# Attention output from float32r products with both parts of the values as 128 weight columns

## The chip, the cores and the metric

The kernel runs on one core of a Trainium2 chip. The metric is the device time of one execution in microseconds. Before the change it was 3017.5 us, the median of three runs (3017.45 to 3017.97). The engines are TensorE (PE; its weight loads are listed apart as PEld), VectorE (DVE), ScalarE (ACT), GpSimd (POOL) and SyncE (SP, which issues the DMAs).

## The reference

The program is a mixing block with a gated delta rule (block 1) and, behind it, a two-layer block (block 2) for 512 tokens of width 1024. Each layer of block 2 is a feed-forward part, a mixer, a second feed-forward part and a gated embedding. The change lies in the mixer's attention, eight heads of width 64:

```python
def forgetting_attention(q, k, v, f_logit):
    b, s, h, dh = q.shape
    scale = 1.0 / float(np.sqrt(dh))
    c = jnp.cumsum(jax.nn.log_sigmoid(f_logit.astype(jnp.float32)), axis=1)
    ...
    for blk in range(s // Q_BLOCK):
        qs, qe = blk * Q_BLOCK, (blk + 1) * Q_BLOCK
        sc = jnp.einsum('bhqd,bhkd->bhqk', qh[:, :, qs:qe], kh[:, :, :qe]).astype(jnp.float32) * scale
        sc = sc + (c[:, :, qs:qe, None] - c[:, :, None, :qe])
        causal = jnp.arange(qs, qe)[:, None] >= jnp.arange(qe)[None, :]
        sc = jnp.where(causal[None, None], sc, -jnp.inf)
        pr = jax.nn.softmax(sc, axis=-1).astype(vh.dtype)
        outs.append(jnp.einsum('bhqk,bhkd->bhqd', pr, vh[:, :, :qe]))
```

Everything is float32. The query block is 128 tokens, so four blocks see 128, 256, 384 and 512 keys. The change concerns the last line, probabilities times values.

## The kernel before

Weight products are made from two-part operands: a float32 matrix is split into hi, its value rounded to float32r, and lo, the rest in float32r, and three float32r matmuls add hi·hi, hi·lo and lo·hi (`mm3`, lines 153 to 158). Weights stream from HBM in the order of their use; ScalarE casts four tiles to `whi` (line 108) and VectorE subtracts to get `wlo` (line 109). A matmul of 512 moving columns into one PSUM bank is the usual piece.

In the mixer the tokens' values are computed first, token-major, in four PSUM banks `v` (lines 499 to 506); ScalarE copies each bank to SBUF in float32 with a scale per token (`vt`, line 509). Then come the forget gates (line 512, their product is `pj`), the first pair's queries and keys, and then `heads` for the four pairs of heads. For a pair it makes, for each of the four query blocks, the scores of both heads `sc` (lines 451, 453, the mask 457), the row maxima (VectorE, line 459), the exponentials (ScalarE, line 461), the reciprocal and the scaling of the probabilities `pe` (VectorE, lines 462, 466). Then, for each of four key blocks, it transposes the probabilities on TensorE into a PSUM bank `pt` (line 476), copies that to SBUF on VectorE (line 480), and multiplies values by them (`o`, line 484). These last products are in plain float32: 64 columns of values are the weights, the transposed probabilities of 512, 384, 256 or 128 queries move, and the two heads write the lower and the upper 64 partitions of one bank. At the end ScalarE and VectorE split the output into `oh` and `ol` (lines 168, 169).

Between these steps stand fillers. `fill(n)` advances the projection of the next pair's queries and keys (`qk_steps`; the last pair has the first of the later gates) by n steps of three weight products, and `taps(n)` gives VectorE n multiply-adds of the depthwise convolution (`cy`, line 418), which nobody needs before the attention is over. The finished order on each engine is settled when the program is built: a scheduler goes through the instructions by their place in the code and by when their operands and buffers are expected to be ready. Each engine then works through its own list in order. PSUM is divided into four banks for accumulators (`acc`: v, pj) and four for the rest (`aux`: sc, pt, and o before the change).

After the four pairs come sixteen gates and the output projections; the attention's output is needed after the first four gates.

Of the kernel before, what the change touches and what calls it, by code (L numbers as in the profile page):

```python
# [7 lines left out]
F32 = mybir.dt.float32  # L8
F32R = mybir.dt.float32r
AF = mybir.ActivationFunctionType  # L10
ALU = mybir.AluOpType
# [12 lines left out]
ENG2 = dict(pe="v", dup="a", pt="vv")  # L24
# [58 lines left out]
class Stream:  # L83
    """Weight tiles in the order of their use: loads of GRP tiles, split in units of UNIT tiles."""
# [40 lines left out]
    def group(self, dst):  # L125
        """the next GRP tiles as they are"""
        assert self.i % GRP == 0
        self.nc.sync.dma_start(dst, self.dram[self.i // GRP])
        self.i += GRP
# [31 lines left out]
def split_scaled(nc, hi, lo, src, scale):  # L161
    """hi + lo == src * scale (scale: a value per partition)."""
    nc.scalar.activation(hi, src, AF.Copy, scale=scale)
    nc.vector.scalar_tensor_tensor(lo, src, scale, hi.bitcast(F32), op0=ALU.mult, op1=ALU.subtract)
# [12 lines left out]
def block2(tc, kk, W, h, xp, x0, sq0, p_t, par, out_t):  # L177
    """h: 8 tiles [128, 512] (features on partitions), short of the factor 1 / rms of the block before.
    x0: the first operand, split. sq0: the sums of squares for that factor and for the first norm."""
    nc = tc.nc  # L180
    with ExitStack() as ctx:
# [23 lines left out]
        # second operands of the scores, double buffered, for the two heads of a pair:  # L205
        # upper q and ones; lower k and both parts of the decay sums
# [9 lines left out]
        # mt[q, k] = NEG where k > q  # L216
# [60 lines left out]
        def token_sums(sq):  # L277
            """means of squares with a token per partition, [128, chunk]"""
# [14 lines left out]
        def spread(r):  # L293
            """from a token per partition to tokens along the free axis of every partition"""
# [6 lines left out]
        def first_norm():  # L301
            """1 / rms of the block before times the first norm's factor; and the former for h"""
# [57 lines left out]
        def mixer(l, after):  # L360
# [8 lines left out]
            def qk_steps(hp, qk1):  # L369
                """for either head: (upper | lower) q and (upper | upper) k"""  # L370
# [56 lines left out]
            def taps(n):  # L427
                """the next n of the products that are possible by now"""
# [7 lines left out]
            def heads(hp, qk1, filler):  # L436
                """heads 2 hp and 2 hp + 1, each in its half of the partitions"""
# [31 lines left out]
                po_ = paux("o")  # L469
                for kb in range(4):  # L470
                    n = S - kb * P
                    pts = []
                    for i in range(2):
# [4 lines left out]
                        t = mtile(8 + kb % 2 * 4 + 2 * i, "pt", F32)[:, :n]  # L478
                        copy = nc.scalar.copy if ENG2["pt"][i] == "a" else nc.vector.tensor_copy
                        copy(t, ps[:, :n])  # L480
                        pts.append(t)
                    fill(FILL[4 + kb])
                    for i, r in enumerate(rr):
                        nc.tensor.matmul(po_[r, kb * P:], lhsT=vt[kb][:, hp * P + 64 * i:hp * P + 64 * i + 64], rhs=pts[i],  # L484
                                         start=kb == 0, stop=kb == 3)
                split(nc, oh[hp], ol[hp], po_)
# [4 lines left out]
            # token sums of squares per partition, for the token-major values  # L491
# [6 lines left out]
            # v, token-major  # L498
# [8 lines left out]
            vt = [mtile(t, f"vt{t}", F32) for t in range(4)]  # L507
            for t in range(4):
                nc.scalar.activation(vt[t], vps[t], AF.Copy, scale=Rt[:, 2 * t:2 * t + 1])
            taps(TAPSV)  # L510
            # forget gates: rows 0..7 and again 64..71
# [9 lines left out]
            # -log_sigmoid = ln(1 + exp(-|z|)) - min(z, 0)  # L521
# [35 lines left out]
            # the merge: gates run ahead of the two parts  # L557
# [96 lines left out]
def blocks(v, n):  # L654
    """[..., n * 128] -> [128, ... * n]"""
# [43 lines left out]
# (shift, scale) blocks that are computed together  # L699
# [98 lines left out]
def block1(tc, kk, W, h, xp, hp, xt, ctxt, par1, po, rcnt, prep2):  # L798
    """Fills h (8 tiles [128, 512]) with the block's output before its final norm is applied, times the
    final gain; prep2(m) is called for each one. Returns the sums of squares for both norms."""  # L800
    nc = tc.nc
    with ExitStack() as ctx:
# [36 lines left out]
        # ---- constants  # L839
# [6 lines left out]
        for d in range(2):  # L846
            t = tmp("tri", (P, P))
            # d = 0: 1 where row <= col; d = 1: 1 where row >= col
# [7 lines left out]
        for b in (16, 32, 64):  # L856
            # -1 on the two off-diagonal blocks of every pair of b x b blocks
# [13 lines left out]
        # row selector: column r picks rows r and 64 + r  # L871
# [17 lines left out]
        # ---- modulation vectors, [128, block, (x, ctx)]  # L889
        # (x, ctx) of every input tile, the last ones filled up to a column tile  # L890
# [4 lines left out]
        # sums over the four column tiles, whose first two rows count  # L895
# [7 lines left out]
        def modulation(bs, tiled, tiles):  # L903
            """four blocks; tiled: with the inputs spread over four column tiles"""
# [19 lines left out]
        # ---- load x, ctx; sums of squares; scale by the reciprocal rms  # L924
# [21 lines left out]
        def newton(r, v, s):  # L946
            """r = 1 / sqrt(v) to float32's accuracy from an estimate r; s: scratch"""
# [80 lines left out]
        # ---- gates: per token on partitions, [128, chunk, 2 directions x 8 heads]  # L1028
# [50 lines left out]
        # ---- per head  # L1079
        # tokens with two columns of zeros around each sequence: ctx from 2 on, x from 260 on  # L1080
# [8 lines left out]
        def conv5(px, pc, blk, dst):  # L1089
            """centred convolution over tokens, then silu; dst: [128, NT + 2] (a gap after ctx) or [128, NX],  # L1090
            None: left in the input's place"""
# [25 lines left out]
        def k_in(hd):  # L1117
# [25 lines left out]
            # gamma and its product with the decay to the chunk's end, [128, chunk, direction]  # L1143
# [19 lines left out]
        def q_in(st):  # L1163
# [10 lines left out]
            # 128 eps (|q|^2 + eps)  # L1174
# [402 lines left out]
```

## Time and profile before

| | before |
|---|---|
| median of the runs | 3017.5 us |
| span of the profiled execution | 3016.3 us |
| TensorE busy | 2970.0 us (98%) |
| VectorE busy | 1916.6 us (64%) |
| ScalarE busy | 1302.3 us (43%) |
| o (L484), chain that ended last | 1% of the span |

The median of the runs is 1.2 us above the profiled span. The busy time of an engine is the sum of the stretches in which it executes; the chain that ended last follows the work back from the last instruction, and shows which engine was waited for. A layer's attention is about 3% of the span, so its own windows say more than the shares of the whole. Time between two starts on an engine is its price when it works without a gap; the time shown for one instruction is longer, since the next begins before it has drained.

### The profile page before, as it was taken

The numbers are of one execution on the slowest core, as the hardware profiler recorded it, in microseconds if no ns is written. First come the engines' busy times: TensorE is split into PE (matmuls) and PEld (weight loads), VectorE is DVE, ScalarE is ACT, GpSimd is POOL, SyncE is SP. The second block draws the span as 40 slices with busy tenths as digits, with TensorE's granted clock in tenths as the row PEclk, the third lists the DMA queues.
The fourth block names the chain that finished last, engine by engine and source line by source line (L and its number), as shares of the span: only waits on it lengthen the run. The fifth ranks groups of instructions, "written<-read, shape, count | busy, mean of one in ns | idle before, by whom it ended". The sixth has DMA issues, their size and how long they took to land.

```text
span 3016.3 us, 37957 instructions
## 1 busy us (share of the span) xinstructions
PE 2970.0 (98%) x13980; PEld 2395.5 (79%) x13980; DVE 1916.6 (64%) x3778; ACT 1302.3 (43%) x2395; POOL 48.4 (2%) x105
## 2 busy tenths in 40 slices
PE   7999999999999999999999999999999999999998
PEld 4888887777888887688888878888887688888886
DVE  5788888777534469886543447434469886543446
ACT  5667666435323335544332335323335544432333
POOL 1000000000000000000000000000000000000000
PEclk9999999999999999999999999999999999999999
DMA  5211113232232232133333333323222123233322
GB/s 199 66 46 45 52 51 110 91 91 89 93 98 97 92 98 78 50 92 97 94 95 98 98 98 93 96 91 98 91 93 89 50 85 98 93 96 98 98 91 84
DMA packets 112971, 268.77 MB, mean 89 GB/s; under 512 B 43537, under 2 KB 47121, under 8 KB 112785
## 3 DMA queue, kind: packets, MB, share of 16 engines
q1 hardware_dynamic: 111760, 266.28, 28.3%
q8 instruction: 110, 1.80, 0.2%
q14 instruction: 77, 0.62, 0.1%
q0 software_dynamic: 1024, 0.07, 0.0%
HBM read 262.17 MB, written 4.06 MB: 88 GB/s over the span
## 4 chain that ended last, share of the span: by engine, by line
PE 95%; DVE 2%; ACT 2%; issue 1%; DMA 0%; DVEq 0%; SPq 0%; ACTq 0%
PE pj L158 17%; PE pj L157 17%; PE pj L156 17%; PE fo L158 5%; PE fo L157 5%; PE fo L156 5%; PE px L156 3%; PE px L157 3%; PE px L158 3%; PE o L484 1%; PE wo L157 1%; PE wo L158 1%; PE mP L1266 1%; PE mX L1261 1%; PE wo L156 1%; PE chn L1313 1%
## 5 line engine op out<-in xcount | busy, mean ns | idle before, releaser
L108 ACT CAST whi<-wraw 128x512 fp32r<-128x512 f32 x914 | 566.6, 620 | 1191.9 <-PE pj L157 712.2
L109 DVE TENSOR_TENSOR wlo<-wraw,whi 128x512 fp32r<-128x512 f32 x914 | 627.1, 687 | 465.9 <-ACT whi L108 441.8
L157 PE MATMUL pj<-xl,whi 128*128 128x512 f32 x1712 | 673.0, 393 | 0.0
L156 PE MATMUL pj<-xh,whi 128*128 128x512 f32 x1712 | 670.7, 392 | 0.9 <-DVE h L1502 0.9
L158 PE MATMUL pj<-xh,wlo 128*128 128x512 f32 x1712 | 670.0, 391 | 0.0
L158 PEld LDWEIGHTS pj<-xh,wlo 128*128 128x128 f32 x1712 | 322.1, 188 | 68.1 <-issue 2.3
L157 PEld LDWEIGHTS pj<-xl,whi 128*128 128x128 f32 x1712 | 322.2, 188 | 67.9 <-issue 2.7
L156 PEld LDWEIGHTS pj<-xh,whi 128*128 128x128 f32 x1712 | 322.4, 188 | 66.8 <-ACT whi L108 1.3
L158 PE MATMUL fo<-gh,wlo 128*128 128x512 f32 x704 | 279.1, 396 | 0.0
L157 PE MATMUL fo<-gl,whi 128*128 128x512 f32 x704 | 279.1, 396 | 0.0
L156 PE MATMUL fo<-gh,whi 128*128 128x512 f32 x704 | 279.0, 396 | 0.0
L418 DVE SCALAR_TENSOR_TENSOR cy<-ca,par,cy 128x489 f32<-128x489 f32 (+17 forms) x240 | 169.6, 729 | 1.5
L157 PE MATMUL px<-xl,whi 128*128 128x512 f32 x392 | 160.4, 409 | 0.0
L158 PE MATMUL px<-xh,wlo 128*128 128x512 f32 x392 | 160.0, 408 | 0.0
L156 PE MATMUL px<-xh,whi 128*128 128x512 f32 x392 | 159.3, 406 | 0.0
L157 PEld LDWEIGHTS fo<-gl,whi 128*128 128x128 f32 x704 | 132.6, 188 | 32.3
L156 PEld LDWEIGHTS fo<-gh,whi 128*128 128x128 f32 x704 | 132.6, 188 | 32.3
L158 PEld LDWEIGHTS fo<-gh,wlo 128*128 128x128 f32 x704 | 132.6, 188 | 32.3
L339 DVE TENSOR_TENSOR fb<-pj,R 128x512 f32<-128x512 f32 x88 | 60.8, 691 | 131.5 <-PE pj L158 131.5
L336 DVE TENSOR_TENSOR fa<-pj,R 128x512 f32<-128x512 f32 x88 | 60.8, 691 | 127.4 <-PE pj L158 125.5
L156 PE MATMUL pj<-nh,whi 128*128 128x512 f32 x352 | 140.0, 398 | 0.0
L157 PE MATMUL pj<-nl,whi 128*128 128x512 f32 x352 | 139.5, 396 | 0.0
(431 smaller groups left out, 4499.0 us busy)
## 6 DMA issues: line engine op xcount, KB each, us to landing
wraw<-in_w_dram SPq DMA_DIRECT2D x465, 512.0 KB
mw<-in_w_dram SPq DMA_DIRECT2D x16, 512.0 KB
raw<-in_xt_dram SPq DMA_DIRECT2D x8, 256.0 KB
h<-in_xt_dram SPq DMA_DIRECT2D x8, 256.0 KB
out_dram<-fin SPq DMA_DIRECT2D x8, 256.0 KB
rawc<-in_ctxt_dram SPq DMA_DIRECT2D x2, 512.0 KB
db<-B SPq DMA_DIRECT2D x64, 6.0 KB
Pm<-dq SPq DMA_DIRECT2D x64, 12.0 KB
```

The lines of the kernel that those rows point to most:

```text
L108: nc.scalar.copy(hi, src)
L109: nc.vector.tensor_tensor(lo, src, hi.bitcast(F32), op=ALU.subtract)
L156: nc.tensor.matmul(ps, lhsT=wh, rhs=xh, start=start, stop=False)
L157: nc.tensor.matmul(ps, lhsT=wh, rhs=xl, start=False, stop=False)
L158: nc.tensor.matmul(ps, lhsT=wl, rhs=xh, start=False, stop=stop)
L336: nc.vector.tensor_tensor(a, pa, R, op=ALU.mult)
L339: nc.vector.tensor_tensor(b, pb, R, op=ALU.mult)
L418: nc.vector.scalar_tensor_tensor(yy[:, s:], ca[cb][:, :S - s], pcol("conv_w", l, cb, j), yy[:, s:], op0=ALU.mult, op1=ALU.add)
L484: nc.tensor.matmul(po_[r, kb * P:], lhsT=vt[kb][:, hp * P + 64 * i:hp * P + 64 * i + 64], rhs=pts[i], start=kb == 0, stop=kb == 3)
L1261: nc.tensor.matmul(pX[:, o], lhsT=st.B[:, m0 + m], rhs=alt(st.Q, m0 + m), start=True, stop=True)
L1266: nc.tensor.matmul(pP[:, o], lhsT=Xt[:, m], rhs=alt(st.P, m0 + m), start=True, stop=True)
L1313: nc.tensor.matmul(pa, lhsT=st.kN[:, c], rhs=y2, start=True, stop=True)
```

## The change

The values are split into two float32r parts while they leave PSUM: for each bank and each of the two heads of a pair, ScalarE writes the hi part and VectorE the lo part of 4 x 64 columns, so that hi and lo of a head lie side by side in 128 columns (line 524 and 525 in the changed file). The transposed probabilities are split too: ScalarE casts the bank to hi, VectorE subtracts to get lo (lines 168, 169) in place of one copy. For each head and key block two float32r matmuls, with the 128 columns as weights and hi, then lo, moving, add up in a bank of the head's own, taken from `acc`. The upper 64 partitions then hold one part's sum and the lower 64 the other's: ScalarE copies one half across (line 488), VectorE adds the other (line 489), and the result is split as before.

```diff
-ENG2 = dict(pe="v", dup="a", pt="vv")
+ENG2 = dict(pe="v", dup="a")
...
-                po_ = paux("o")
+                po_ = [psum(f"o{i}") for i in range(2)]
...
-                        t = mtile(8 + kb % 2 * 4 + 2 * i, "pt", F32)[:, :n]
-                        copy = nc.scalar.copy if ENG2["pt"][i] == "a" else nc.vector.tensor_copy
-                        copy(t, ps[:, :n])
+                        t = [mtile(8 + kb % 2 * 4 + 2 * i + j, "pt")[:, :n] for j in range(2)]
+                        split(nc, t[0], t[1], ps[:, :n])
                         pts.append(t)
                     fill(FILL[4 + kb])
-                    for i, r in enumerate(rr):
-                        nc.tensor.matmul(po_[r, kb * P:], lhsT=vt[kb][:, hp * P + 64 * i:hp * P + 64 * i + 64], rhs=pts[i],
-                                         start=kb == 0, stop=kb == 3)
-                split(nc, oh[hp], ol[hp], po_)
+                    for i in range(2):
+                        for j in range(2):
+                            nc.tensor.matmul(po_[i][:, kb * P:], lhsT=v2(kb, 2 * hp + i), rhs=pts[i][j],
+                                             start=kb == 0 and j == 0, stop=kb == 3 and j == 1)
+                t = tmp("ov")
+                for i, r in enumerate(rr):
+                    nc.scalar.copy(t[r], po_[i][rr[1 - i]])
+                    nc.vector.tensor_tensor(t[r], t[r], po_[i][r], op=ALU.add)
+                split(nc, oh[hp], ol[hp], t)
...
-            vt = [mtile(t, f"vt{t}", F32) for t in range(4)]
+            vt = [[mtile(2 * t + i, f"vt{t}{i}") for i in range(2)] for t in range(4)]
+            def v2(t, hd):
+                return vt[t][hd % 2][:, hd // 2 * P:hd // 2 * P + P]
...
             for t in range(4):
-                nc.scalar.activation(vt[t], vps[t], AF.Copy, scale=Rt[:, 2 * t:2 * t + 1])
+                for i in range(2):
+                    b = vt[t][i].rearrange("p (a s c) -> p a s c", s=2, c=64)
+                    hi, lo = b[:, :, i], b[:, :, 1 - i]
+                    src = vps[t].rearrange("p (a e c) -> p a e c", e=2, c=64)[:, :, i]
+                    sc = Rt[:, 2 * t:2 * t + 1]
+                    nc.scalar.activation(hi, src, AF.Copy, scale=sc)
+                    nc.vector.scalar_tensor_tensor(lo, src, sc, hi.bitcast(F32), op0=ALU.mult, op1=ALU.subtract)
```

The rest of the file's changes are comments. The order of the instructions moves with it, at three places above all.

TensorE in the first layer's last pair, around the first product of the output. `pj` is a weight product of a gate (filler), `pt` a transpose, `o` the output. Before:

```order
L156 MATMUL pj<-xh_10082,whi 128x512
L157 MATMUL pj<-xl_10083,whi 128x512
L158 MATMUL pj<-xh_10082,wlo 128x512
L156 MATMUL pj<-xh_10138,whi 128x512
L157 MATMUL pj<-xl_10139,whi 128x512
L476 MATMUL pt<-ident,pe 128x128
L158 MATMUL pj<-xh_10138,wlo 128x512
L156 MATMUL pj<-xh_10190,whi 128x512
L476 MATMUL pt<-ident,pe 128x128
L157 MATMUL pj<-xl_10191,whi 128x512
L158 MATMUL pj<-xh_10190,wlo 128x512
L484 MATMUL o<-pt,vt_10944 64x512 x2
```

The same place of the changed kernel; the first row is the last weight product ahead of it.

```order
L158 MATMUL pj<-xh_10414,wlo 128x512
L457 MATMUL sc<-maskr,identr 128x128 x2
L451 MATMUL sc<-qk_11899,qk_11732 128x512
L453 MATMUL sc<-k_7750,q_7749 128x512
L457 MATMUL sc<-maskr,identr 128x128
L451 MATMUL sc<-qk_11905,qk_11736 128x512
L453 MATMUL sc<-k_7752,q_7751 128x512
L457 MATMUL sc<-maskr,identr 128x128
L476 MATMUL pt<-ident,pe 128x128 x12
L484 MATMUL o_12034<-pt,vt_10944 128x512
L476 MATMUL pt<-ident,pe 128x128 x2
L484 MATMUL o_12034<-pt,vt_10944 128x512
```

No weight product is left between the last scores and the output; twelve transposes follow the scores directly. Counted over a layer, 189 weight products stood between the first score and the last o (44, 47, 49 and 49 for the pairs), and 148 stand there now (27, 49, 48 and 24).

ScalarE between the second and the third pair of the first layer. `qk` is a cast of the third pair's keys, `ov` the new copy of half an output bank, `pe` an exponential. Before:

```order
L108 CAST whi<-wraw 128x512
L380 CAST qk_11559<-qk 64x512
L393 CAST qk_11559<-qk 64x512
L380 CAST qk_11565<-qk 64x512
L108 CAST whi<-wraw 128x512
L393 CAST qk_11565<-qk 64x512
L168 CAST oh_10431<-o 128x512
L461 ACTIVATE pe,sm<-sc,sm 128x128 x2
```

And now:

```order
L168 CAST pt<-pt 128x128 x2
L488 COPY ov<-o_11524 64x512
L488 COPY ov<-o_11525 64x512
L380 CAST qk_11635<-qk 64x512
L393 CAST qk_11635<-qk 64x512
L380 CAST qk_11641<-qk 64x512
L108 CAST whi<-wraw 128x512
L168 CAST oh_10431<-ov 128x512
L393 CAST qk_11641<-qk 64x512
L461 ACTIVATE pe,sm<-sc,sm 128x128 x2
```

The casts of the next pair's keys stood ahead of the output's end; they now stand behind two copies that read the finished output.

ScalarE where the values leave PSUM, first layer; `v_10804` is the first bank, which the forget gates' product takes next. Before:

```order
L509 ACTIVATE vt_10944<-v_10804,Rt 128x512
L509 ACTIVATE vt_10945<-v_10805,Rt 128x512
L509 ACTIVATE vt_10946<-v_10806,Rt 128x512
L108 CAST whi<-wraw 128x512
L509 ACTIVATE vt_10947<-v_10807,Rt 128x512
```

And now:

```order
L524 ACTIVATE vt_10944<-v_10804,Rt 128x4x64
L524 ACTIVATE vt_10946<-v_10805,Rt 128x4x64
L524 ACTIVATE vt_10948<-v_10806,Rt 128x4x64
L108 CAST whi<-wraw 128x512
L524 ACTIVATE vt_10945<-v_10804,Rt 128x4x64
L524 ACTIVATE vt_10950<-v_10807,Rt 128x4x64
```

The first bank is read last by the fifth of these and by a VectorE instruction behind it, where one copy read it before.

## Rows read from the trace of the kernel before

**Rows 1.** The page's chain that ended last, shares by engine.

```profile
PE 95%; DVE 2%; ACT 2%; issue 1%; DMA 0%; DVEq 0%; SPq 0%; ACTq 0%
```

**Rows 2.** Windows, first score to last o: length; PE, PEld, DVE, ACT, POOL busy; clock; DMA.

```profile
1185.76:1277.09 91.33, 90.29 (x429) 61.99 (x429) 81.49 (x194) 51.17 (x115) 3.84 (x8) 0.96 0.18 53
2323.74:2414.11 90.37, 88.95 (x429) 60.57 (x429) 81.31 (x194) 51.04 (x115) 3.85 (x8) 0.98 0.17 53
```

**Rows 3.** Windows again: first row maximum to last copied block, either layer.

```profile
1188.39:1276.17 87.78, 86.74 (x415) 59.24 (x415) 78.11 (x190) 48.69 (x112) 3.84 (x8) 0.98 0.17 50
2326.38:2413.19 86.81, 85.77 (x412) 58.26 (x411) 77.92 (x190) 48.55 (x112) 3.85 (x8) 0.98 0.16 50
```

**Rows 4.** Windows of line 484 (o) alone: PE, PEld, clock, DMA.

```profile
1185.76:1277.09 91.33, 17.14 (x64) 4.80 (x64) 0.96 0.18 53
```

**Rows 5.** Timeline of TensorE, full clock: start, us, engine, line, operation, shapes.

```profile
1236.44 0.34 PE L453 MATMUL sc<-k,q 66*128 66x384 f32 x1
1236.62 0.40 PE L156 MATMUL pj<-xh,whi 128*128 128x512 f32 x1
1236.86 0.39 PE L157 MATMUL pj<-xl,whi 128*128 128x512 f32 x1
...
1256.07 0.28 PE L453 MATMUL sc<-k,q 66*128 66x256 f32 x1
1256.19 0.39 PE L157 MATMUL pj<-xl,whi 128*128 128x512 f32 x1
```

**Rows 6.** Timeline of TensorE, o in the third pair (two records a product).

```profile
1251.04 0.87 PE L484 MATMUL o<-pt,vt 128*64 128x384 f32 x4
...
1252.20 0.65 PE L484 MATMUL o<-pt,vt 128*64 128x256 f32 x2
```

**Rows 7.** Lines by form, VectorE, first layer's attention: count, busy, mean ns.

```profile
L480 DVE COPY pt<-pt 128x512 f32<-128x512 f32 x8 | 5.3, 684 | 0.3
...
L466 DVE TENSOR_SCALAR pe<-pe,sm 128x512 f32<-128x512 f32 x8 | 3.8, 479 | 0.0
L480 DVE COPY pt<-pt 128x256 f32<-128x256 f32 x8 | 3.3, 418 | 0.8 <-PE pt L476 0.7
...
L169 DVE TENSOR_TENSOR ol<-o,oh 128x512 fp32r<-128x512 f32 x3 | 2.1, 689 | 1.4 <-ACT oh L168 1.4
```

**Rows 8.** Lines by form, ScalarE, first layer's attention.

```profile
L461 ACT ACTIVATE pe<-sc,sm 128x256 f32<-128x256 f32 x8 | 3.7, 470 | 1.4 <-DVE sm L459 1.4
...
L168 ACT CAST oh<-o 128x512 fp32r<-128x512 f32 x4 | 2.3, 587 | 20.8 <-PE o L484 20.8
```

**Rows 9.** Timeline of VectorE: taps, subtractions of 64x512, a gate scaling.

```profile
1187.10 1.38 DVE L418 SCALAR_TENSOR_TENSOR cy<-ca,par,cy 128x484 f32<-128x484 f32 x2
1188.39 0.48 DVE L459 TENSOR_REDUCE sm<-sc 128x1 f32<-128x128 f32 x2
...
1202.81 1.39 DVE L385 TENSOR_TENSOR k<-qk,qk 64x512 fp32r<-64x512 f32 x2
...
1267.39 0.67 DVE L535 TENSOR_TENSOR ga<-pj,R 128x512 f32<-128x512 f32 x1
1267.98 0.68 DVE L109 TENSOR_TENSOR wlo<-wraw,whi 128x512 fp32r<-128x512 f32 x1
```

**Rows 10.** Timeline of ScalarE where the values leave PSUM.

```profile
1160.89 2.05 ACT L509 ACTIVATE vt<-v,Rt 128x512 f32<-128x512 f32 x3 [0.28 <-PE v L506]
1162.84 0.61 ACT L108 CAST whi<-wraw 128x512 fp32r<-128x512 f32 x1
```

**Rows 11.** Timeline of TensorE: the forget gates' first product.

```profile
1162.73 0.39 PE L156 MATMUL pj<-xh,whi 128*128 128x512 f32 x1
```

**Rows 12.** Timeline of TensorE: the first scores of the first layer.

```profile
1185.76 0.47 PE L451 MATMUL sc<-qk,qk 128*128 128x128 f32 x1 [2.01 <-ACT qk L393]
...
1186.56 0.63 PE L156 MATMUL pj<-xh,whi 128*128 128x512 f32 x1
```

**Rows 13.** Windows: the first layer's first pair, granted clock third from the end.

```profile
1185.80:1211.00 25.20, 25.20 (x112) 18.22 (x113) 21.60 (x50) 14.47 (x32) 1.92 (x4) 0.87 0.19 64
```

## The prediction

> **What bounds the kernel now.** I read the chain that ended last first: TensorE holds 95% of it, nearly all of it weight products, and the attention output (o, L484) 1% [rows 1]. So a change pays only where TensorE itself gets shorter, and it costs wherever it makes TensorE wait. The change touches two places in each of the two layers, so the second view is the window of the attention: from the first score to the last o of a layer 91.3 and 90.4 us [rows 2]. In it TensorE is busy nearly throughout, but VectorE is too: between the first row maximum and the last copy of a transposed probability it works 78.1 of 87.8 us and 77.9 of 86.8 us [rows 3]. That is 89%, with 9.7 and 8.9 us free. TensorE stays busy there only because weight products of later steps are spread between the scores, the transposes and o. The reader should see two engines close to full in one stage, kept apart by this filler.
>
> **What becomes shorter.** o occupies TensorE 17.1 us in a layer [rows 4]. Afterwards a pair of heads needs four products of each width: 512 columns at 0.23 us start to start, 384 at 0.18, 256 at 0.12, and 128 at no more than 0.12 [rows 5], so 4 x 0.65 = 2.6 us, 10.4 us for the four pairs. That is 6.7 us less work per layer. Part of the 17.1 us is waiting: where both heads' copies are ready, four records (two products) of 384 columns take 0.87 us together, hardly more than one product of 256 columns alone, 0.65 us [rows 6]; the two 64-column halves run side by side. The Trainium skill's page TensorEngine Tiling (section Key Properties) says that tiles run matmuls in parallel, and (Theoretical Speedup) up to twofold for 64 columns. The trace agrees where both start together. By that rule alone every pair of products would cost what [rows 6] shows, 0.87 x 1280 / 384 = 2.9 us for a pair of heads, and the change would save 0.3 us there; it speaks against the change, though in this forecast it only shrinks the first rival.
>
> **What is added on VectorE and ScalarE.** A transposed block was one VectorE copy; now it is a ScalarE cast and a VectorE subtraction. The copies cost 684 ns at 512 columns and 418 at 256, a subtraction from PSUM of 512 columns 689 ns [rows 7], so I take them as equal at every width. The eight casts and two copies a pair are new on ScalarE, 587 ns at 512 columns [rows 8] and less at the narrower ones: at most 5.9 us a pair, 24 us a layer, beside the 48.7 of 87.8 us that ScalarE works today [rows 3]. It has room. New on VectorE are two additions of 64x512 per pair. Their nearest row is two subtractions of that shape in 1.39 us, 0.70 each [rows 9].
>
> Then the order decides, which is written out ahead of the run. From a layer's first row maximum to its last block of probabilities VectorE had 188 instructions and now has 194: six additions more (the last pair's come later), 21 conv taps become 27, 16 weight remainders become 12, and one q/k scaling and one gate scaling fall behind the end. At 0.70 an addition, 0.65 a tap (two in 1.29 us start to start) and 0.59 for each of the others (a gate scaling to the next start) [rows 9] that is 4.2 + 3.9 - 2.4 - 0.6 - 0.6 = +4.5 us. TensorE does less in the same stretch: 148 filler products until the last o in place of 189 (27, 49, 48 and 24 for the four pairs; 44, 47, 49 and 49 before). The 41 that are missing come afterwards, at 0.23 us: 9.4 us in a stage where TensorE has no gap to hide them. So a TensorE that was filled behind VectorE is no longer filled; in the last pair nothing but transposes stands between scores and o, and the wait for softmax is bare. That is the term the forecast rests on.
>
> **The attention, added up.** VectorE's work in the stretch becomes 78.1 + 4.5 = 82.6 us (82.4 in the second layer). How much of its idle time stays is unknown: none, or all 9.7 and 8.9 us. I step through the second pair by hand, each instruction at its price and after what it waits for. From the first head's last scaled probability to the last o: a reciprocal, a tap, a weight remainder, a scaling (1.7 us), eight subtractions (3.2 us), two taps (1.3 us), against some 6.7 us for the whole. From there to the next pair's first maximum: scaling of k 0.6, additions 1.4, lower parts of k 1.4, remainders 1.2, 4.6 us of about 5.1; here ScalarE's two new copies wait for the last o, and behind them stand the casts of k that the next scores need. In the rest VectorE has no gap in either order. So about 0.8 us stay free per pair; for four I take 3. A layer's stretch, first score to last o, is then 2.6 (up to the first maximum, as now) + 82.6 + 3 + 0.4 = 88.6 us, and 88.4. Plus 9.4 us of deferred products, less 91.3 and 90.4: +6.7 and +7.4 us, together +14.1. With no idle time it is +8; with all of today's +27.
>
> **The values.** Today four ScalarE copies empty the four banks of v; the first starts at 1160.89 and three take 2.05 us [rows 10]. The first bank is free near 1161.6, and the forget gates' first product, which needs it, starts at 1162.73 without a wait [rows 11]. Afterwards a bank is free when both its halves have been cast and subtracted. ScalarE's order is: half of bank one, of two, of three, a weight cast, then the other half of bank one. The weight cast starts at 1162.84 [rows 10] and takes 0.6; the half takes at most what a 256-column exponential does, 470 ns [rows 8]: 1163.8. VectorE has the remainder of that weight cast ahead (until 1164.05), then the subtraction, 256 columns like a copy's 418 ns [rows 7]: 1164.45. TensorE waits 1.7 us, 3.5 us for two layers. Bounds are 0 (if a bank's first half already freed it) and 2.5 us a layer. Nothing hides it: that product is next on TensorE, and the forget gates behind it lead to the first scores, before which TensorE waits 2.01 us today already [rows 12].
>
> **At no cost.** The weights come in the same order and the DMA engines are 17% busy [rows 3], so SyncE's queue does not matter; GpSimd's row copies keep their place. The o accumulators move into the weight products' four banks; they are emptied 2.4 us after the last o, and the next holder starts later.
>
> **Sum.** 3017.5 + 14.1 + 3.5 = 3035.1 us. The profiled span is 3016.3 us and the median of the runs 1.2 us more, so I add to the median: 3035 us. The unknown costs alone (no idle time and no wait for the values; all of today's idle time and 2.5 us a layer) bound it by 3025.6 and 3049.2 us.
>
> **Rivals.**
> *VectorE doesn't set the pace.* Then the 6.7 us of o are saved in both layers and the values cost 3.5: 3017.5 - 13.4 + 3.5 = 3007.6 us. For it: idle waits on both engines today. Against: 89% busy, and 4.5 us more work against 9.7 us free while the filler is gone. 6%.
> *Subtracting is cheaper than copying, and VectorE never idles.* A scaling of 512 columns in SBUF takes 479 ns [rows 7], 0.2 less than a copy; if the subtractions, with one operand in SBUF, cost that, the 32 of a layer save some 0.1 us each in the mean, 3.3 us: 3017.5 + 8 - 6.6 + 2 (the values, cheaper too) = 3020.9 us. For it: the taps that came forward fill today's gaps. Against: the 689 ns of [rows 7]. 11%.
> *The clock falls.* Before the first scores TensorE stood 2.01 us, a 512-column product right behind shows 0.63 us, and in the stretch that begins there the granted clock is 0.87 on average [rows 12, 13]: it fell from 2.4 to 1.2 GHz for a part. The bare wait of the last pair, some 5 us with a few transposes, is longer. If the clock falls there, and in one more pair, and TensorE comes back slow, each fall costs what such a stretch costs today, about 25.2 x 0.13 = 3.3 us, less what lies behind VectorE; one to two in a layer give 3042 to 3048 us. The Trainium skill's TensorE: Matmul & The Clock Gate (section The HAM clock gate) says that an idle engine drops to half rate and work brings it back; the fall in [rows 12, 13] agrees. 17%.
> *The forecast,* 66%.
>
> **Chances.** 0.2%, 6 us, is about what can be told from no change. Faster by more 6%, within 11%, slower 83%. The range reaches from the cheaper subtractions to the upper bound, which two falls of the clock a layer also stay under: 3021 to 3050 us.
>
> **What would show it.** Right: in both layers first score to last o in 86 to 92 us with VectorE over 92% busy, TensorE idle 20 us or so there, a wait of 1.5 to 2 us ahead of the forget gates' product, and in the last pair no weight product from the scores to o. Wrong: VectorE idle as today with the stretch beyond 93 us (the casts' latency then sets the pace), or the last o more than 10 us earlier than now.

## The result, and the profile after the change

The changed kernel took 3041.39 us (median of four runs, 3038.41 to 3042.30) beside 3017.47 for the kernel before: ratio 1.0079, 95% interval 1.0066 to 1.0092. It is 23.9 us slower; 17.5 were forecast. The third experiment below turned out to be the same program with the same instruction order, so there are nine runs of it in all, 3038.4 to 3042.3 with 3039.7 in the middle. Experiments are measured against that 3039.7 where a few us matter; by it the change costs 22.2 us.

Both profiled executions, cut at the same instructions (first and second layer):

| stretch, us | before | changed | forecast, both layers | measured, both layers |
|---|---|---|---|---|
| last product of the values to the forget gates' product | 0.23, 0.23 | 2.25, 2.25 | +3.5 | +4.1 |
| from there to the first score | 23.02, 23.02 | 24.64, 24.66 | 0 | +3.3 |
| first score to last o | 91.33, 90.37 | 90.72, 90.60 | -4.7 | -0.4 |
| from there to the next layer's values, or the last product | 1001.75, 593.15 | 1010.31, 601.70 | +18.8 | +17.1 |

The profiled execution of the changed kernel, 3042.3 us, is the slowest of the nine. In the profile of the third experiment, the same program at 3038.8 us, the four rows come to +4.1, +0.1, -0.6 and +17.0 us.

The windows from the first score to the last o (length, then busy us of TensorE, its weight loads, VectorE, ScalarE, GpSimd, the granted clock as a share of full, DMA), beside [rows 2]:

```profile
1189.48:1280.20 90.72, 79.06 (x387) 60.72 (x388) 83.98 (x199) 63.00 (x148) 3.83 (x8) 0.94 0.13 42
2339.09:2429.68 90.59, 78.75 (x387) 60.17 (x388) 84.14 (x199) 62.89 (x148) 3.84 (x8) 0.94 0.13 42
```

The same from the first row maximum to the last block of probabilities, beside [rows 3]:

```profile
1192.02:1279.96 87.94, 76.54 (x373) 58.51 (x372) 81.37 (x196) 60.70 (x145) 3.83 (x8) 0.94 0.12 37
2341.60:2429.35 87.75, 76.17 (x373) 57.92 (x371) 81.47 (x195) 60.62 (x145) 3.84 (x8) 0.94 0.12 37
```

The stretch is as long as it was, but the full engine has changed. TensorE was busy for 90.29 of 91.33 us and is now busy for 79.06 of 90.72; VectorE went from 78.1 of 87.8 to 81.4 of 87.9. The weight products in the stretch fell from 189 to 148 in either layer. Two of the missing ones now stand ahead of the first score, 39 behind the last o; at 0.227 us from start to start these are 8.9 us, and the stage behind grew by 8.6.

VectorE's waits in the first layer's stretch (us in all, how many, the longest):

```profile
DVE pt L169 <- ACT pt L168: 2.8, 5, 1.2
DVE sm L462 <- ACT pe L461: 1.5, 2, 1.3
DVE wlo L109 <- ACT whi L108: 0.8, 2, 0.4
DVE k L385 <- ACT qk L380: 0.4, 2, 0.2
```

And VectorE's instructions there by form (line, tiles, shapes, count; busy us and mean ns; idle us before them and who ended it):

```profile
L169 DVE TENSOR_TENSOR pt<-pt 128x512 fp32r<-128x512 f32 x8 | 5.5, 688 | 0.7 <-ACT pt L168 0.5
L169 DVE TENSOR_TENSOR pt<-pt 128x384 fp32r<-128x384 f32 x8 | 4.3, 546 | 0.0
L489 DVE TENSOR_TENSOR ov<-ov,o 64x512 f32<-64x512 f32 x6 | 4.1, 679 | 0.1
L169 DVE TENSOR_TENSOR pt<-pt 128x256 fp32r<-128x256 f32 x8 | 3.2, 422 | 2.3 <-ACT pt L168 2.3
```

A subtraction costs what the copy did: 688 and 422 ns against 684 and 418 in [rows 7]. That leaves nothing of the rival with cheaper subtractions. The additions are new.

TensorE in the first layer's last pair (start, duration, line, tiles, shapes, count, idle before it in brackets):

```profile
1266.85 0.22 PE L457 MATMUL sc<-maskr,identr 128*128 128x128 f32 x1
1270.21 1.00 PE L476 MATMUL pt<-ident,pe 128*128 128x128 f32 x4 [3.13 <-ACT pe L461]
1271.44 2.27 PE L476 MATMUL pt<-ident,pe 128*128 128x128 f32 x8 [0.23 <-ACT pe L461]
1274.17 0.80 PE L484 MATMUL o<-pt,vt 128*128 128x512 f32 x1 [0.46 <-ACT pt L168]
```

From the last mask to the first transpose TensorE stands for 3.13 us, as no weight product is left. Then the clock is down, at 0.50 of full from 1271.27 us on: eight transposes take 2.27 us, 0.28 each with the small gaps between them, and a product of 512 columns 0.80 us. The window of that fall, and ahead of it that of an earlier one, which the next paragraphs explain:

```profile
1165.45:1168.86 3.41, 3.41 (x10) 2.67 (x9) 2.23 (x6) 0.93 (x3) 0.00 (x0) 0.50 0.00 0
1271.27:1278.10 6.83, 6.15 (x20) 4.31 (x21) 5.07 (x13) 3.07 (x9) 0.00 (x0) 0.50 0.00 0
```

The place where the values leave PSUM, on ScalarE and then on VectorE:

```profile
1162.83 0.62 ACT L108 CAST whi<-wraw 128x512 fp32r<-128x512 f32 x1
1163.35 0.83 ACT L524 ACTIVATE vt<-v,Rt 128x256 fp32r<-128x256 f32 x2
```

```profile
1163.61 0.68 DVE L109 TENSOR_TENSOR wlo<-wraw,whi 128x512 fp32r<-128x512 f32 x1
1164.21 2.43 DVE L525 SCALAR_TENSOR_TENSOR vt<-v,Rt,vt 128x256 fp32r<-128x256 f32 x6
```

The first bank's second half is cast behind a weight cast and subtracted behind that weight's remainder, from 1164.21; it then takes some 0.45 us. So TensorE starts the forget gates at 1164.84, and what follows could not be read from the trace before:

```profile
1162.58 0.39 PE L510 MATMUL v<-wlo,xh 128*128 128x512 f32 x1
1164.84 0.47 PE L156 MATMUL pj<-xh,whi 128*128 128x512 f32 x1 [1.87 <-DVE vt L525]
...
1166.16 0.63 PE L157 MATMUL pj<-xl,whi 128*128 128x512 f32 x1
1166.58 0.63 PE L158 MATMUL pj<-xh,wlo 128*128 128x512 f32 x1
```

Behind the wait, from 1165.73 us on, eight weight products start 0.43 us apart in place of 0.23: TensorE runs at 1.2 GHz, half its clock, for 3.41 us. The only other gap of that segment is one of 1.46 us ahead of the first score. The fall costs 1.6 us a layer and is nearly all of the 3.3 us in the table's second row.

### The profile page after: what moved, and what is told of

The parts are those of the page before. It is cut to its first block, busy times and chain, and to the rows that moved or that the text cites. A ratio compares the mean times of both kernels' runs of the same rounds, so it can differ in the third digit from the quotient of the medians.

```text
span 3040.6 us, 38049 instructions
## 1 busy us (share of the span) xinstructions
PE 2971.5 (98%) x13980; PEld 2413.8 (79%) x13980; DVE 1931.8 (64%) x3810; ACT 1337.1 (44%) x2483; POOL 48.4 (2%) x105
## 5 line engine op out<-in xcount | busy, mean ns | idle before, releaser
L418 DVE SCALAR_TENSOR_TENSOR cy<-ca,par,cy 128x491 f32<-128x491 f32 (+18 forms) x240 | 170.8, 728 | 1.3
L158 PE MATMUL pj<-nh,wlo 128*128 128x512 f32 x352 | 139.7, 397 | 0.0
```

The source lines that it names most:

```text
L158: nc.tensor.matmul(ps, lhsT=wl, rhs=xh, start=False, stop=stop)
L418: nc.vector.scalar_tensor_tensor(yy[:, s:], ca[cb][:, :S - s], pcol("conv_w", l, cb, j), yy[:, s:], op0=ALU.mult, op1=ALU.add)
```

## Experiments

**1. Free the banks of the values at once.**

```
-    nc.scalar.activation(hi, src, AF.Copy, scale=sc)             # src: the PSUM bank
-    nc.vector.scalar_tensor_tensor(lo, src, sc, hi.bitcast(F32), op0=ALU.mult, op1=ALU.subtract)
+    nc.scalar.activation(vf, vps[t], AF.Copy, scale=sc)          # one copy a bank; src: its halves in vf
...
+    nc.scalar.copy(hi, src)
+    nc.vector.tensor_tensor(lo, src, hi.bitcast(F32), op=ALU.subtract)
```

> The changed kernel, but each bank of values is first copied by one scaled ScalarE instruction to SBUF, as before the change, and split into hi and lo from there. Theory A (the first bank is held until its second half has been cast and subtracted, and the 1.87 us in which TensorE stands there also lets its clock fall for the ten weight products behind, which start every 0.43 us in place of 0.23): the wait ahead of the forget gates' product is gone, from the last product of the values to that one 0.2 us in place of 2.25, from there to the first scores about 23.0 us in place of 24.65, both layers: 2 x (2.0 + 1.6) = 7 us less than the changed kernel, about 3034. Rival B (the wait alone costs; what follows is late for its own reasons, such as the longer row of ScalarE work): the 2.0 us go, 24.65 stays: 4 us less, about 3037. Rival C (the split of the values is late for the forget gates or the first product of the output in either order): no gain.

Measured: 3035.23 us (3034.64 to 3036.43), ratio to before 1.0060 (1.0047 to 1.0072). TensorE no longer waits:

```profile
1162.12 0.39 PE L510 MATMUL v<-wlo,xh 128*128 128x512 f32 x1
1162.35 0.39 PE L156 MATMUL pj<-xh,whi 128*128 128x512 f32 x1
```

The first segment is back at 0.23 us, and forget gates to first score takes 23.45 us with one weight product more in it than the changed kernel has. The total is 6.2 us less than the changed kernel's own median, 4.5 less than the middle of its nine runs. The wait's 4.1 us are shown; how much of the rest was the clock, the next two runs tell.

**2. Fill the wait with products.**

```
+    du = paux("du")
+    for d in range(8):
+        nc.tensor.matmul(du, lhsT=wh[:, 0:P], rhs=xh[7], start=d == 0, stop=d == 7)
```

> The changed kernel with eight more products of 512 columns on TensorE between the last product of the values and the forget gates' first product; nobody reads their result. At 0.23 us each they fill 1.8 us, just the wait that is there. Theory A (the clock falls because TensorE stands still): last product of the values to the forget gates' product stays 2.1 to 2.4 us, but the granted clock stays at full rate behind it, and forget gates to first scores takes 22.6 to 23.2 us in place of 24.65: 3.3 to 4 us less in all, about 3038. Rival B (the fall has another cause, or what it costs is given back at the wait ahead of the first scores): 24.6 us again, and within 1 us of the changed kernel.

Measured: 3038.61 us (3038.21 to 3039.45). The segments were 2.05 and 23.01 us with full clock behind, as theory A has it. But the next run shows 23.05 us with the wait left bare, so this one alone decides nothing on the cause.

**3. No taps in the pairs (as intended).** `TAPS1 = (1, 1, 2, 1)` became `(0, 0, 0, 0)`.

> The changed kernel without convolution taps inside the four pairs; they are made later, among the gates. 27 taps of 0.65 us, 17.5 us a layer, leave VectorE's 81.4 us in the attention. Theory A (VectorE sets the pace there): first score to last output product falls from 91 us to 80 to 85 us, where TensorE (79 us of work) or the latency of single steps takes over; if the taps find room later, 12 to 20 us less in all, about 3025; if VectorE is then late for the convolution's output, part of it is given back. Rival B (the latency of casts, exponentials and transposes sets the pace and VectorE's work only fills the time): the stretch stays over 88 us and the total is within 4 us of the changed kernel, or above it.

Measured: 3039.02 us (3038.58 to 3041.97). The edit did nothing: the scheduler fetched the 27 taps forward again, and the order on every engine is the changed kernel's, buffer names aside. What it gives is a second profile of that program:

```profile
1164.89 0.47 PE L156 MATMUL pj<-xh,whi 128*128 128x512 f32 x1 [1.87 <-DVE vt L525]
...
1165.67 0.39 PE L156 MATMUL pj<-xh,whi 128*128 128x512 f32 x1
1165.89 0.39 PE L157 MATMUL pj<-xl,whi 128*128 128x512 f32 x1
```

The same wait of 1.87 us, and no fall behind it: 23.05 us to the first score in both layers against 24.64 and 24.66. The clock of the stretch behind it, first layer:

```profile
1165.67:1168.20 2.53, 2.53 (x13) 2.08 (x12) 2.07 (x5) 1.20 (x3) 0.00 (x0) 1.00 0.00 0
```

So a wait of this length may or may not be followed by the fall, and where it is, it costs 1.6 us here. Between this profiled execution and that of experiment 1, neither with this fall, lie 4.1 us, as much as the wait. All profiles together point to the wait as the cause: where the wait stands bare (the changed kernel, experiments 3, 4 and 12, two layers each) the clock fell behind it in five of eight places; where it is gone, filled or shorter (the kernel before and the other nine experiments) it fell between the last product of the values and the first score in none of twenty. The Trainium skill's page TensorE: Matmul & The Clock Gate (section The HAM clock gate) says that the monitor behind the clock runs freely, so that the moment of a change differs from run to run. Two executions of one program, one with the fall and one without, fit that.

**4. More filler for the last pair.** `GATES0 = 1` became `2`.

> The changed kernel with two gates, not one, as the filler of the last pair: 24 more weight products stand between its scores and its output, 5.4 us of TensorE work, with a scaling and two weight remainders (2 us) more on VectorE. Theory A (the last pair's waits are bare, and weight products put there cost nothing): the stretch grows by at most 2 us, 5.4 us a layer leave the stage behind it, and the clock does not fall in the last pair, which gives back 1 to 2 us: 3.4 to 6 us a layer, 7 to 12 in all, about 3032. Rival B (VectorE is full there too, or the products delay the transposes): the stretch grows by as much as leaves the later stage, within 3 us of the changed kernel.

Measured: 3027.83 us (3026.30 to 3030.73), ratio 1.0034 (1.0021 to 1.0048).

```profile
1190.44:1280.59 90.15, 81.76 (x411) 63.06 (x412) 84.92 (x201) 64.07 (x150) 3.82 (x8) 0.98 0.15 48
2334.01:2424.18 90.17, 81.80 (x412) 63.06 (x412) 84.90 (x201) 64.08 (x150) 3.85 (x8) 0.98 0.15 48
```

24 more products stand in a stretch that is 0.5 us shorter, the clock is 0.98 in place of 0.94, and the stage behind lost 5.5 and 6.3 us. That is theory A: the last pair's wait was bare, and more work on TensorE cost nothing there. 12 us came from it, half the loss.

**5. Taps really held back.** `TAPS1` is at zeros as in experiment 3, and three one-column instructions behind the last pair's output (`ca + 0 * ol`, in which the value doesn't change) make the later convolution inputs wait for it.

```
+    if hp == 3:
+        for b in (ca[1], ca[2], ca[3]):
+            nc.vector.scalar_tensor_tensor(b[:, 0:1], ol[3][:, 0:1].bitcast(F32), 0.0, b[:, 0:1],
+                                           op0=ALU.mult, op1=ALU.add)
```

> The changed kernel with the convolution taps held back until the last pair's output is split (three one-column instructions make the convolution's inputs wait for it), so that none can stand in the pairs. VectorE loses 27 taps of 0.65 us, 17.5 of its 81.4 us between a layer's first row maximum and its last split block. Theory A (VectorE sets the pace there): first score to last output product falls from 91 us to 80 to 85 us, and the total by 10 to 20 us, to 3021 to 3031, unless the taps are then late for the convolution's output. Rival B (the latency of casts, exponentials, transposes and products in a row sets the pace): the stretch stays over 88 us, and the total within 4 us of the changed kernel.

Measured: 3042.17 us (3040.47 to 3043.72), ratio 1.0084 (1.0071 to 1.0098).

```profile
1184.36:1271.23 86.87, 78.55 (x397) 61.94 (x398) 70.16 (x172) 63.41 (x149) 3.96 (x9) 0.94 0.15 43
2334.07:2418.81 84.74, 76.19 (x397) 60.02 (x398) 70.11 (x172) 63.46 (x149) 3.96 (x9) 0.98 0.14 45
```

The stretch is 3.9 and 5.9 us shorter although ten more products stand in it, 2.3 us, which stood ahead of the first score before. ScalarE's work is as it was (63.4 us for 63.0). So VectorE's work did set the pace, as theory A has it, but 14 us less of it gave 4 to 6: the rest became waiting, 11.7 us of it in the first layer for ScalarE's casts and exponentials. All of the gain was given back, the exception that theory A named: the stage behind is 8.4 and 9.0 us longer, and the convolution's output is late there:

```profile
PE pj L156 <- ACT yh L168: 6.4, 1, 6.4
```

**6. Experiment 1 with three gates.** `GATES0 = 3`, and in the last pair `FILL = (4, 5, 4, 1, 2, 3, 3, 2)`.

> The changed kernel with the copied values of the first experiment and three gates, not one, as the filler of the last pair (FILL there 4, 5, 4, 1, 2, 3, 3, 2). From what the two gave apart, 6.2 us for the values and 13.6 us for the second gate, 3021.6 us. The third gate moves 24 more weight products, 5.4 us, into the last pair, and the built order has 34 taps in the attention in place of 27. Theory A (TensorE's idle time of 8.4 us a layer that the second gate left can still take products for nothing): 3 to 5 us less per layer, 3011 to 3016. Rival B (VectorE is full, so the seven taps and a gate's own work, 6 us, lengthen the stretch by about what leaves the later stage): 3019 to 3024.

Measured: 3028.56 us (3028.16 to 3029.13), more than either theory gave. Experiment 8 shows where it was lost.

**7. Experiment 6 with the taps of experiment 5.**

> The sixth kernel (copied values, three gates) with the taps held back as in the fifth: VectorE has room, and TensorE has 48 more weight products, 10.9 us, among the pairs than in the changed kernel. Theory A (VectorE set the pace, and TensorE takes it over): first score to last output product 86 to 90 us with TensorE busy for over 95% of it; against the changed kernel 6 us for the values, 2 x 10.9 for the products that leave the later stage and 2 to 8 for the shorter stretch: 3005 to 3013, less than the kernel before. Rival B (latency sets the pace): the stretch at 91 us or more and 3014 to 3022. If the taps are late for the convolution's output, the stage behind grows by what they lack there.

Measured: 3054.02 us (3052.46 to 3054.88), the slowest of all, and both theories missed it. The stretch is 94.5 and 97.0 us, TensorE busy for 93% of it, and the stage behind is 17 us longer than in experiment 6:

```profile
1184.09:1278.61 94.52, 87.47 (x444) 68.77 (x445) 72.11 (x176) 67.41 (x155) 3.82 (x8) 0.98 0.17 49
2338.41:2435.43 97.02, 90.05 (x445) 71.00 (x445) 72.21 (x176) 67.53 (x155) 3.83 (x8) 0.95 0.16 48
```

TensorE's waits in the stage behind, second layer:

```profile
PE pj L156 <- ACT yh L168: 9.0, 1, 9.0
PE ssps L259 <- DVE ysq L591: 4.3, 1, 4.3
```

The taps have a due time: where all of them leave the pairs, they stand in front of the convolution's output.

**8. Experiments 1 and 4 together.**

> The changed kernel with the copied values of the first experiment and the two gates of the fourth, and no other edit. Theory A (the two cures are independent): 6.2 and 13.6 us less than 3041.4, 3021.6 us, within 2 us; the sixth kernel's 3028.6 is then the price of its third gate and seven more taps, 7 us. Rival B (what is gained at the values or by the second gate is lost again in the pairs, because VectorE is full there): 3026 us or more.

Measured: 3022.98 us (3022.04 to 3025.24), ratio 1.0020 (1.0011 to 1.0029). The two add up: 3039.7 - 4.5 - 11.9 = 3023.3. First layer of this kernel, and below it of experiment 6:

```profile
1185.29:1275.27 89.98, 83.52 (x410) 64.10 (x411) 85.05 (x201) 64.18 (x150) 3.84 (x8) 0.96 0.13 48
```

```profile
1186.52:1284.34 97.82, 90.62 (x432) 69.31 (x433) 92.07 (x211) 66.89 (x154) 3.83 (x8) 0.95 0.15 47
```

The third gate and eight more taps gave VectorE 7.0 us more, and the stretch grew by 7.8, more than the products took from the stage behind (5.0 and 5.6 us). Whether VectorE's work alone did that is not shown: TensorE has 7.1 us more as well, and experiment 7, with 20 us less on VectorE than experiment 6, is only 3.3 and 1.1 us shorter with twelve more products. With three gates TensorE is near its limit too.

**9. Experiment 8 with the probabilities scaled on ScalarE** (`ENG2 = dict(pe="a", dup="a")`), and the next taps held back as in 5, from the point in the convolution that has been reached by then.

> The eighth kernel with the scaling of the probabilities (11.9 us a layer) on ScalarE in place of VectorE, and the next convolution taps held back behind the last pair, so that 13 taps stand in the attention, not 27: VectorE's work there goes from about 83 to about 62 us, ScalarE's from 62 to about 75. Theory A (VectorE set the pace and TensorE takes it over): first score to last output product 84 to 88 us in place of 90 to 91, the stage behind pays up to 4 us a layer for 14 late taps, as part of the 8.4 and 9.0 that 27 cost: 3010 to 3019 us. Rival B (the scaling lies behind each exponential on ScalarE, whose row is then the longest chain): the stretch 90 us or more, 3022 to 3032.

Measured: 3023.58 us (3023.26 to 3029.48). First layer, the clock at full, and VectorE's largest wait in it:

```profile
1186.66:1277.00 90.34, 81.63 (x410) 61.33 (x411) 70.31 (x155) 77.56 (x182) 3.83 (x8) 1.00 0.15 47
```

```profile
DVE sm L465 <- ACT pe L464: 8.6, 17, 1.2
```

That is rival B. VectorE has 15 us less to do than in experiment 8 and waits 8.6 us for exponentials that stand behind scalings on ScalarE. The profiled execution was the slowest of nine. Its second layer took 96.0 us at a clock of 0.91; what made it fall more there stays open.

**10. Only the second head's scaling on ScalarE.**

```
-    if ENG2["pe"] == "a":
+    if i == 1:
         nc.scalar.activation(pe, pe, AF.Copy, scale=sm[:, 2:3])
```

> As the ninth kernel, but only the second head's probabilities are scaled on ScalarE: VectorE about 68 us, ScalarE about 69 in the attention. Theory A (the fuller of the two sets the pace until TensorE does): first score to last output product 83 to 87 us, a little shorter than the ninth's, 3008 to 3017 us. Rival B (latency of single steps, whatever the engines' load): the stretch 90 us or more, 3022 to 3030.

Measured: 3011.25 us (3010.76 to 3012.40), ratio to before 0.9980 (0.9971 to 0.9989).

```profile
1185.58:1270.69 85.11, 81.24 (x412) 64.08 (x413) 73.69 (x171) 70.91 (x166) 3.83 (x8) 0.96 0.15 50
2320.32:2404.67 84.35, 79.34 (x413) 61.55 (x413) 73.42 (x171) 70.69 (x166) 3.82 (x8) 1.00 0.16 51
```

That is theory A. With 73.7 and 70.9 us on the two engines TensorE is the fullest again, and the stretch is 6 us shorter than before the change, though with 173 weight products in place of 189, for which the stage behind pays 2.5 and 2.1 us. It is the only version that beats the kernel before.

**11. The same relief without the change** (experiment 10's two edits on the kernel before).

> The kernel before the change with what the tenth kernel does for VectorE: the second head's probabilities scaled on ScalarE, the next convolution taps held back behind the last pair (8 taps and a start stand among the pairs in place of 20 and one). VectorE's work among the pairs goes from 78 to about 64 us. Theory A (before the change TensorE is idle for 1.0 to 1.4 us of the pairs' 91, so VectorE had little left to give there): within 3 us of the kernel before, 3014 to 3020, and the tenth kernel's gain needs the changed output. Rival B (the relief is worth as much without the change): 3009 to 3013.

Measured: 3020.11 us (3018.10 to 3021.95), ratio 1.0009 (1.0000 to 1.0018): no gain, as theory A has it (0.1 us above its range).

```profile
1185.84:1274.08 88.24, 85.89 (x417) 57.01 (x418) 68.11 (x162) 57.79 (x130) 3.86 (x8) 1.00 0.16 49
```

In this first layer the stretch gets 3.1 us shorter, but with 178 products in place of 189, and the stage behind pays 2.7. TensorE had next to nothing idle that could be taken out. A second gate beside the relief was not tried on the kernel before; TensorE is idle for 2.4 and 1.7 us of the two stretches here. An estimate from that, if all of it took products, is 3016 us, still above experiment 10.

**12. The relief alone on the changed kernel** (experiment 10's two edits, values and gate as changed).

> The changed kernel with the relief of VectorE alone, as in the tenth (second head's probabilities scaled on ScalarE, taps held back: 12 in the attention in place of 27), the values and the single gate as they were. VectorE's work between the first row maximum and the last split block goes from 81.4 to about 66 us, ScalarE's from 61 to about 68. Theory A (VectorE sets the pace of the changed kernel's pairs): first score to last output product falls from 91 to 82 to 86 us with the same 149 weight products, the stage behind loses up to 4 us of it to late taps, 3022 to 3034 us. Rival B (the relief helps only together with the second gate's products): the stretch 89 us or more, 3038 to 3044.

Measured: 3029.02 us (3028.72 to 3031.91), ratio 1.0042 (1.0028 to 1.0055).

```profile
1189.05:1274.49 85.44, 76.22 (x388) 59.35 (x388) 72.49 (x167) 70.41 (x164) 3.84 (x8) 0.96 0.15 44
2331.70:2416.89 85.19, 75.57 (x388) 58.77 (x388) 72.31 (x167) 70.28 (x164) 3.85 (x8) 0.96 0.14 44
```

The same 148 products take 5.3 and 5.4 us less, while the stage behind stayed at 1010.3 and 600.9 us (601.7 in the changed kernel): fifteen taps that came later cost nothing there. The two stretches together lost 10.7 us, as much as the median lies below 3039.7. VectorE has 11.5 us less to do and ScalarE 7.4 more, so it was VectorE's work that held the stretch. Less than half of the relief came out as time, and no engine is over 90% busy now; what sets the pace then was not settled. The three cures add up: 3039.7 - 4.5 - 11.9 - 10.7 = 3012.6, and experiment 10, which has all three, took 3011.3.

## Why the prediction was right, and what it mis-sized

**The mechanism was right.** VectorE paces the changed kernel's pairs: less work on it shortens the stretch (experiments 5 and 12), more work on TensorE does not lengthen it (experiment 4). The filler that TensorE had there is deferred and paid for behind (experiment 4), and the values hold the forget gates' product up (experiment 1). Of the five marks it named four came true: 90.7 and 90.6 us, VectorE at 92.6% of the stretch, a wait of 1.87 us, and no weight product from the last scores to the last pair's first o. TensorE's idle time did not. The four rows of the table missed by +0.6, +3.3, +4.3 and -1.7 us, so a small part of the misses cancelled by luck.

**The deferred products** were forecast at 9.4 us a layer and measured at 8.6: two of the 41 went ahead of the first score, where TensorE had been waiting, and the price is 0.227, not 0.23.

**The stretch** was forecast at 88.6 and 88.4 us. VectorE's work came out 1.1 us smaller than I had it (81.4 for 82.5), but I left it 3 us of idle time and it has 6.6 and 6.3. The hand walk through the second pair was carried over to all four, and the first and the last are different: 1.3 us for one exponential in the first, and in the last 1.7 for ScalarE's casts, which follow transposes at half clock. The first layer's waits, 5.5 us in all, are 2.6 in the first pair, 0.6 in the second, 0.6 in the third and 1.7 in the last. In experiment 4, where the clock holds in the last pair, its 1.7 are 0.4; that run also has products in the wait, so the clock's share is not shown apart. The stretch's miss is 4.3 us for both layers.

**The values** were forecast at 1.7 us a layer. The wait was right (1.87 us, 2.02 counted from start to start), but I ended the account there. Behind it the clock fell in the profiled execution, 1.6 us a layer more, which the sum put at nothing. My rival on the clock looked for the fall in the last pair; it came there too (0.94 for the stretch, 0.96 and 0.98 in [rows 2]), where a part of it lies behind VectorE. The measured time lies between the forecast and that rival's 3042: VectorE set the pace as forecast, and the clock fell as the rival had it.

**What TensorE saves in o** was wrong, without harm to the sum since TensorE wasn't what paced the stretch. I set 17.1 us of busy time before against 10.4 us from start to start after. By the same view the changed o takes this, in experiment 10's second layer at full clock:

```profile
2320.32:2404.67 84.35, 16.41 (x64) 10.41 (x64) 1.00 0.16 51
```

16.4 against 17.1 in [rows 4], so 0.7 us saved, not 6.7. Counted from each start to the next, it is 15.9 before and 13.5 here, 2.4 us saved: beside transposes the next start often comes some 0.1 us later than [rows 5] shows for products in a row. Two places of the last pair there, a product ahead of a weight product and one ahead of transposes, 0.23 and 0.34 us to the next start:

```profile
2399.62 0.39 PE L487 MATMUL o<-pt,vt 128*128 128x512 f32 x1
2399.85 0.40 PE L158 MATMUL pj<-xh,wlo 128*128 128x512 f32 x1
...
2400.16 0.50 PE L487 MATMUL o<-pt,vt 128*128 128x512 f32 x1
2400.50 0.49 PE L479 MATMUL pt<-ident,pe 128*128 128x128 f32 x3
```

The Trainium skill's rule that the prediction weighed against the change (page TensorEngine Tiling, section Theoretical Speedup: up to twice as fast where a dimension is 64 or less) gave 0.3 us a pair, 1.2 a layer; that was nearer to either count than my sum. So the first rival's 3007.6 was out of reach; with VectorE relieved and both other costs cured the kernel stands at 3011.

**TensorE's idle time** was expected near 20 us and is 11.7 a layer. The 20 do not follow from the prediction's own terms: 90.3 us of work less 9.4 for the products and 6.7 for o are 74.2 of 88.6 us, which leaves 14.4. TensorE's busy time then came out 4.9 us longer than that, with o's real price and the half clock in it, and the stretch 2.1.

## What to carry to other kernels

A faster product helps only as far as the engines that prepare its operands have room: count what the splits, copies and extra sums add on the engines that empty PSUM before counting columns, and take both sides of a saving from the same view. Where a scheduler places the filler, look in the built order at which waits stay bare, and at how much each engine has left in that stage. Where two engines empty PSUM for a third, try more than one division of the work. Here VectorE and ScalarE at 73.7 and 70.9 us gave a stretch of 85.1, 85.1 and 64.2 (with more taps) gave 90.0, and 70.3 and 77.6 gave 90.3. Equal shares as such were not tested: the three also differ in what stands behind each exponential.

## What the runs showed of the hardware

- The same instructions in the same order took 3038.4 to 3042.3 us over nine runs. In one profiled execution TensorE's granted clock fell to 0.50 behind a wait of 1.87 us, which cost 1.6 us; in another, behind the same wait, it did not. Over all profiles it fell in five of eight places with this wait, and in none of twenty without it.
- Subtracting a float32r tile in SBUF from a float32 bank in PSUM costs VectorE what a copy of that bank does: 688, 546, 422 and 281 ns at 512, 384, 256 and 128 columns in the changed kernel, against 684, 551, 418 and 287 for the copies in the kernel before.
- Two float32 products of 64 weight columns side by side (four records) and the four float32r products of 128 columns that replace them take nearly the same busy time on TensorE at full clock, 17.1 us a layer (before) and 16.4 (experiment 10).
